# First norm's gain and bias applied beside the third and seventh expert tile, and the experts' load order computed ahead of the gates

## The chip, the cores and the metric

The kernel runs on one core of a Trainium2 chip. The metric is the device time of one execution in microseconds (us), from the first to the last instruction and what little lies around them. Engines are named as in the profile: PE (TensorE, matrix products), DVE (VectorE), ACT (ScalarE), POOL (GpSimd), SP (SyncE, which issues the weight transfers). They run side by side and wait for each other only through semaphores.

## The reference

One layer of a decoder for 512 tokens of width 1024. Four mixing branches are gated and summed into `merged`, and then:

```python
        x = layer_norm(DEEPNORM_ALPHA * x + merged @ w_out[l], ln1_g[l], ln1_b[l])

        y = hierarchical_moe(x.reshape(b * T, D_MODEL), r_group[l], r_group_b[l], r_expert[l],
                             r_expert_b[l], e_gate[l], e_up[l], e_down[l])
        x = layer_norm(DEEPNORM_ALPHA * x + y.reshape(b, T, D_MODEL), ln2_g[l], ln2_b[l])
```

`layer_norm` subtracts the mean, divides by the root of the variance plus 1e-5, and applies a row of gains and a row of biases. `hierarchical_moe` picks one of 4 expert groups for each token and in it the best 2 of 8 experts; an expert computes `silu(x @ w_gate) * (x @ w_up) @ w_down` with matrices of 1024 x 512, 1024 x 512 and 512 x 1024 in float32, and a token's two results are added with gate weights. All 32 experts are read, 6 MB each.

## The kernel before

The first 720 us or so compute the input projection, the four branches, the output product and the first norm. `x1`, which later is called `acc`, is a 512 x 1024 tile in SBUF (four blocks of 128 tokens); `normed` leaves in it the normed rows without gain and bias, and `xh` and `xl` hold the same numbers transposed, rounded (`xh`) and the rest (`xl`).

Then comes the expert stage (`moe`). The experts are worked on in 13 tiles of 128 slots. Tiles 0 and 1 hold the fixed experts 0 to 3, 64 slots each; tiles 2 to 12 are filled by the table `TILES` (rank of an expert by its number of tokens, and its slots), so which expert stands where is known only once the tokens are counted. `router` works that out: it ranks the 28 other experts by their counts (`rkey`, `rsq`, `rrank`), finds each token's slot, and writes the list of experts in the order of the tiles, `R.order` (`rord`). SP reads this list into registers (`num`, line 1188) before it can issue a weight transfer for tile 2 or later.

Weights come in transfers of 1 MB, which I number through: an expert has 6 (two each of gate, up, down), so tile 0 has transfers 0 to 11, tile 1 has 12 to 23, tile 2, with four experts, 24 to 47. There are 16 buffers; transfer n goes into buffer n mod 16 and so waits until PE has read transfer n - 16. All are issued by SP in this order (line 1753), and SP also waits at line 1753 for landings of earlier ones.

A tile is one call of `expert_block`: gate products `pg`, up products `pu`, `hh` = silu(pg) * pu (ACT, then DVE), four transposes, down products `py` from `hT`; `yh` (ACT) and `yl` (DVE) are py scaled and split; `combine` spreads them to the token rows with a one-hot matrix and adds the result to `acc` (DVE, line 1148). A tile's two combines run inside the next tile (`mid` after the gate products, and `late` after hT). `early` and `late` are hooks ahead of and behind the transposes: in tile 0, `early` computes the gates (`gates`, `slot_gates`), then `affine`, and `late` runs `rest`, that is `router`. Every second tile gathers the token columns for the next two (`Gather`, lines 1058 and 1060, into `xe`) with one-hot matrices `D` from the slots.

`affine` turns `acc` into ALPHA * (gain * x + bias): four DVE instructions of 128 x 1024 (line 1873), one ACT instruction (1875), four POOL instructions of 128 x 1024 (1877). Its rows `g1` and `b1` are broadcast to 128 partitions by two transfers of 512 KB from POOL's queue. They stand at the end of `early` in tile 0, so on DVE ahead of tile 0's `hh`, and `router` stands behind it. Instructions are recorded and put in order per engine by a scheduler; `issue_after` holds a group back until an instruction named is issued.

Of the kernel before, what the change touches and what calls it, by code (L numbers as in the profile page):

```python
# [17 lines left out]
P = 128  # L18
# [691 lines left out]
def branch_a(K, st, q, k, v1, v2, v3, emit):  # L710
# [62 lines left out]
    for ct in range(2):  # L773
# [128 lines left out]
def gates(K, R):  # L902

    V, A = K.nc.vector, K.nc.scalar
    sb = K.rwk
    s4 = lambda n: sb.tile([P, 4], F32, name=n)
    bc = lambda t, n: t.unsqueeze(2).to_broadcast([P, 4, n])
    gl = R.lg[:, :, 0:4]
    gm, m1, m2 = (R.m[:, i] for i in range(3))
    ge = sb.tile([P, 4, 4], F32, name="rge")  # L910
    V.tensor_tensor(ge, gl, bc(gm, 4), op=OP.subtract)
    A.activation(ge, ge, AF.Exp)
    gs = s4("rgs")
    V.tensor_reduce(gs, ge, axis=AX.X, op=OP.add)
    e2 = s4("re2")
    V.tensor_tensor(e2, m2, m1, op=OP.subtract)
    A.activation(e2, e2, AF.Exp)
    den = s4("rden")
    V.scalar_tensor_tensor(den, e2, 1.0, gs, op0=OP.add, op1=OP.mult)
    R.g = [K.rsb.tile([P, 4], F32, name=f"rgt{j}") for j in range(2)]  # L920
    V.reciprocal(R.g[0], den)
    V.tensor_tensor(R.g[1], R.g[0], e2, op=OP.mult)


def router(K, R):

    nc = K.nc
# [10 lines left out]
    V.scalar_tensor_tensor(key, cnt[:, ds_], float(NE), K.iof[:, ds_], op0=OP.mult, op1=OP.subtract)  # L938
    sq = sb.tile([P, ND, ND], F32, name="rsq", tag="rsq", bufs=1)
    V.tensor_tensor(sq, key[:, None, :].to_broadcast([P, ND, ND]), key.unsqueeze(2).to_broadcast([P, ND, ND]),  # L940
                    op=OP.is_gt)
    rank = row("rrank", ND)
    V.tensor_reduce(rank, sq, axis=AX.X, op=OP.add)

    at = lambda: V.tensor_tensor(sq, rank[:, None, :].to_broadcast([P, ND, ND]),
                                 K.plan[:, 0].unsqueeze(2).to_broadcast([P, ND, ND]), op=OP.is_equal)
    at()
    V.tensor_tensor(sq, sq, K.plan[:, 1].unsqueeze(2).to_broadcast([P, ND, ND]), op=OP.mult)
    V.tensor_reduce(key, sq.rearrange("p q e -> p e q"), axis=AX.X, op=OP.add)

    base, cap = row("rbase"), row("rcap")
    V.tensor_scalar(base[:, 0:NS], K.iof[:, 0:NS], float(CAP), None, op0=OP.mult)
# [33 lines left out]
    V.tensor_tensor(o8, over.unsqueeze(2).to_broadcast([P, NE, 8]), K.thr[:, None, :].to_broadcast([P, NE, 8]),
                    op=OP.is_gt)
    V.tensor_reduce(nbk, o8, axis=AX.X, op=OP.add)
# [88 lines left out]
            self.evac(h, xe)  # L1077


def expert_block(K, xe, gts, w, ex, out_acc, parts=((0, T), (T, DM)), done=None, spare=None, mid={}, fill=()):  # L1080

# [55 lines left out]
    def combine(i, c0, c1, yh, yl):  # L1137
        for b in range(NB):
            ps = psm.tile([P, c1 - c0], F32, name="pm", padded_shape=[P, T])
            TE.matmul(ps, DT[:, b, :], yh, start=True, stop=False)  # L1140
            end = TE.matmul(ps, DT[:, b, :], yl, start=False, stop=True)  # L1141
            o = out_acc[:, b, c0:c1]
            if spare is not None and (b, i) in POOLED:
                s = spare[0][:, POOLED.index((b, i)) % 8, 0:c1 - c0]
                A.copy(s, ps)  # L1145
                G.tensor_tensor(o, o, s, op=OP.add)  # L1146
            else:
                V.tensor_tensor(o, o, ps, op=OP.add)  # L1148
# [29 lines left out]
    nc.vector.tensor_tensor(lo, src, hi.bitcast(F32), op=OP.subtract)  # L1178


def moe(K, xh, xl, out_acc, R, d0, affine, rest, load, load_rows, load_cols, small, last, ews):

# [76 lines left out]
    for pr, tl in enumerate(tiles):  # L1259
# [233 lines left out]
def layer_kernel(tc, a, out):  # L1493
# [12 lines left out]
    with top:  # L1506
# [362 lines left out]
        K.osb = K.rsb  # L1869

        def affine():
            for b in range(NB):
                V.scalar_tensor_tensor(acc[:, b, :], acc[:, b, :], ALPHA, g1, op0=OP.mult, op1=OP.mult)
            with tc.issue_after(K.xend):
                A.mul(b1, b1, ALPHA)
            for b in range(NB):
                G.tensor_tensor(acc[:, b, :], acc[:, b, :], b1, op=OP.add)
            rst.close()

        def rest():  # L1880
            with ExitStack() as st:
                K.rwk = pool(st, "rw2")
                router(K, R)
# [63 lines left out]
```

## Time and profile before

| | us |
|---|---|
| median of 3 runs | 1215.8 (1214.27 to 1218.3) |
| the profiled execution | 1214.3 |
| its span | 1212.5 |
| PE busy | 1133.9 (94%) |
| DVE busy | 644.4 (53%) |
| ACT busy | 350.3 (29%) |
| POOL busy | 140.2 (12%) |

The profile is of one execution. Times inside it count from the first instruction; the execution's own time is 1.8 us more than its span. In the page's 40 slices the DMA engines are busy in changing amounts up to about 740 us and full from about 760 to 1180 us, at 420 GB/s or so. PE is busy almost throughout, which for pipelined products does not mean that it sets the pace. Weight transfers are asynchronous: SP issues them in order, and a transfer that can't be issued yet holds back all those behind it.

### The profile page before, as it was taken

What the parts mean: (1) busy time and instruction counts of PE and PEld (TensorE: products, weight loads), DVE (VectorE), ACT (ScalarE), POOL (GpSimd) and SP (SyncE); (2) the same over time, 40 slices, a digit from 0 to 9 for tenths busy, and PEclk for the clock granted to TensorE, in tenths of its full rate; (3) what the DMA queues carried; (4) which work ended last, traced back from release to release, by engine and by line L of the source; (5) the groups of instructions that cost most, each with busy time, mean ns of one, the idle gap of its engine ahead of it and who ended that gap; (6) DMA issues with size and microseconds to landing.
All of it is one profiled execution on the core that took longest, in us unless ns stands there. A gap on an engine that the chain in (4) does not pass through costs nothing.

```text
span 1212.5 us, 19047 instructions
## 1 busy us (share of the span) xinstructions
PE 1133.9 (94%) x7039; PEld 761.9 (63%) x7039; DVE 644.4 (53%) x1785; ACT 350.3 (29%) x752; POOL 140.2 (12%) x194
## 2 busy tenths in 40 slices
PE   8999999999999999999999988999999998898882
PEld 6768778888876667888888973533444442442431
DVE  6489788622248884343435589732444442243237
ACT  5434444433343544232334450100111110110012
POOL 4022232000000001111121134000000000000003
PEclk9999999999999999999999998999999998999996
DMA  7320230566561024555554256999999999999992
GB/s 189 84 56 18 54 89 19 157 190 193 179 182 36 18 82 154 169 178 173 160 163 129 71 178 281 415 421 421 420 421 420 420 422 421 420 422 420 421 378 79
DMA packets 108699, 276.65 MB, mean 228 GB/s; under 512 B 19393, under 2 KB 74780, under 8 KB 86076
## 3 DMA queue, kind: packets, MB, share of 16 engines
q1 hardware_dynamic: 90604, 252.79, 56.3%
q10 hardware_dynamic: 16768, 19.82, 5.1%
q0 software_dynamic: 1232, 2.81, 0.7%
q8 instruction: 56, 0.92, 0.3%
q14 instruction: 39, 0.32, 0.1%
HBM read 263.71 MB, written 11.67 MB: 227 GB/s over the span
## 4 chain that ended last, share of the span: by engine, by line
PE 59%; DMA 28%; DVE 9%; issue 1%; ACT 1%; POOL 1%; SPq 0%; ACTq 0%; DVEq 0%; POOLq 0%
DMA w<-in_e_gate 10%; PE mm L1404 9%; PE mm L1406 9%; PE mm L1405 9%; DMA w<-in_e_down 9%; DMA w<-in_e_up 8%; PE pu L1095 2%; PE pg L1095 1%; PE py L1125 1%; PE mm L1424 1%; PE mm L1426 1%; PE mm L1425 1%; PE po L1730 1%; PE po L1728 1%; PE po L1729 1%
## 5 line engine op out<-in xcount | busy, mean ns | idle before, releaser
L1178 DVE TENSOR_TENSOR wlo<-wraw,whi 128x512 fp32r<-128x512 f32 (+2 forms) x180 | 122.3, 683 | 201.2 <-ACT whi L1175 200.5
L1404 PE MATMUL mm<-xh,whi 128*128 128x512 f32 x496 | 198.1, 400 | 1.0 <-ACT whi L1175 0.7
L1405 PE MATMUL mm<-xl,whi 128*128 128x512 f32 x496 | 198.8, 401 | 0.0
L1406 PE MATMUL mm<-xh,wlo 128*128 128x512 f32 x496 | 198.0, 400 | 0.0
L1175 ACT CAST whi<-wraw 128x512 fp32r<-128x512 f32 (+2 forms) x180 | 109.7, 612 | 204.9 <-PE mm L1405 133.3
L1148 DVE TENSOR_TENSOR acc<-acc,pm 128x512 f32<-128x512 f32 (+1 forms) x106 | 64.2, 655 | 116.3 <-PE pm L1141 116.3
L1095 PE MATMUL pu<-w,xe 128*32 128x512 f32 (+1 forms) x576 | 108.0, 632 | 10.9 <-DMA w<-in_e_up 10.9
L1095 PE MATMUL pg<-w,xe 128*32 128x512 f32 (+1 forms) x576 | 103.7, 609 | 11.1 <-DMA w<-in_e_gate 11.1
L1125 PE MATMUL py<-w,hT 128*32 128x512 f32 (+2 forms) x608 | 107.4, 577 | 3.8 <-DMA w<-in_e_down 3.5
L1404 PEld LDWEIGHTS mm<-xh,whi 128*128 128x128 f32 x496 | 93.3, 188 | 26.1 <-issue 3.0
L1406 PEld LDWEIGHTS mm<-xh,wlo 128*128 128x128 f32 x496 | 93.3, 188 | 24.3 <-issue 3.6
L1405 PEld LDWEIGHTS mm<-xl,whi 128*128 128x128 f32 x496 | 93.3, 188 | 22.6 <-issue 2.7
L1095 PEld LDWEIGHTS pg<-w,xe 128*32 128x32 f32 (+1 forms) x576 | 30.7, 124 | 80.1 <-issue 57.4
L1095 PEld LDWEIGHTS pu<-w,xe 128*32 128x32 f32 (+1 forms) x576 | 29.8, 127 | 81.4 <-issue 60.6
L1125 PEld LDWEIGHTS py<-w,hT 128*32 128x32 f32 (+1 forms) x608 | 34.4, 123 | 67.9 <-issue 53.5
L1058 PE MATMUL pm<-D,xh 128*128 128x256 f32 (+1 forms) x224 | 53.9, 283 | 1.1 <-DVE D L1019 1.1
L1146 POOL TENSOR_TENSOR acc<-acc,yo 128x256 f32<-128x256 f32 x6 | 4.3, 732 | 434.0 <-ACT yo L1145 434.0
L1060 PE MATMUL pm<-D,xl 128*128 128x256 f32 (+1 forms) x224 | 53.8, 283 | 0.0
L1102 DVE TENSOR_TENSOR hh<-hh,pu 128x512 f32<-128x512 f32 x13 | 8.9, 686 | 81.1 <-PE pu L1095 81.1
L1735 POOL TENSOR_TENSOR mT<-mT,th 128x512 f32<-128x512 f32 x24 | 35.6, 1485 | 140.9 <-DVE th L1734 139.9
L1133 ACT ACTIVATE yh<-py,dg 128x512 fp32r<-128x512 f32 x24 | 16.5, 686 | 105.7 <-PE py L1125 88.6
L1426 PE MATMUL mm<-whi,xl 128*128 128x256 f32 (+1 forms) x160 | 46.3, 289 | 0.0
(639 smaller groups left out, 2005.2 us busy)
## 6 DMA issues: line engine op xcount, KB each, us to landing
w<-in_e_gate SPq DMA_DIRECT2D x60, 1024.0 KB, 19.8
w<-in_e_down SPq DMA_DIRECT2D x58, 1024.0 KB, 19.8
w<-in_e_up SPq DMA_DIRECT2D x58, 1024.0 KB, 19.8
wraw<-in_w_in SPq DMA_DIRECT2D x128, 256.0 KB, 3.1
w<-in_e_up SPq DMA_DIRECT2D x12, 512.0 KB, 15.7
w<-in_e_down SPq DMA_DIRECT2D x12, 512.0 KB, 8.5
wraw<-in_w_branch SPq DMA_DIRECT2D x16, 256.0 KB, 2.6
w<-in_e_gate SPq DMA_DIRECT2D x8, 512.0 KB, 5.4
```

The costliest lines, as they stand in the source:

```text
L1058: TE.matmul(ps[:, i, :], self.xh[:, kt, b * P:b * P + P], D[:, b, :], start=i == 0 and b == 0, stop=False, skip_group_check=True)
L1060: TE.matmul(ps[:, i, :], self.xl[:, kt, b * P:b * P + P], D[:, b, :], start=False, stop=i == per - 1 and b == NB - 1, skip_group_check=True)
L1095: end = TE.matmul(ps[c, :], xe[:, kt, c], w(e, kind, kt, 0, T), start=kt == 0, stop=kt == 7, skip_group_check=True)
L1125: TE.matmul(at(c0, c1)[c, :], hT[:, f, c], w(e, 2, f, c0, c1), start=f == 0 and c0 % T == 0, stop=f == 3 and c1 % T == 0, skip_group_check ...
L1148: V.tensor_tensor(o, o, ps, op=OP.add)
L1175: nc.scalar.copy(hi, src)
L1178: nc.vector.tensor_tensor(lo, src, hi.bitcast(F32), op=OP.subtract)
L1404: TE.matmul(ps[i], hi[:, k, cs], self.xh[:, kk, :], start=kk == 0, stop=False)
L1405: TE.matmul(ps[i], hi[:, k, cs], self.xl[:, kk, :], start=False, stop=False)
L1406: end = TE.matmul(ps[i], lo[:, k, cs], self.xh[:, kk, :], start=False, stop=kk == 7)
L1426: TE.matmul(ps[:, :n], self.xl[:, kk, s], hi[:, k, :], start=False, stop=kk == 7)
L1735: G.tensor_tensor(mT[:, j, :], mT[:, j, :], th, op=OP.add)
```

## The change

`affine` goes. The load order becomes a function of its own, `load_order`, which runs on DVE right behind the first gather's evacuation (`xe`) and ahead of the gates; `router` keeps the rest, its passes over 28 x 28 cut into two halves of 14 x 28. The first tile's combine writes `acc` with ACT copies in place of DVE additions (`first`). The residual ALPHA * (gain * x + bias) is added in two halves of columns by `residual`, in the `late` hooks of tiles 2 and 6: PE spreads gain and bias to 128 partitions in PSUM, DVE rebuilds x from `xh` and `xl`. Gain and bias are read as a tile of 8 x 256 (`gb8`), by two transfers of 4 x 256 on POOL's queue in place of the two broadcasts. The pool of the router's small tiles opens once, for both functions.

```diff
+RESIDUAL = (2, 6)
+
...
+def at_place(K, R, sq, places=slice(0, ND)):
+
+    K.nc.vector.tensor_tensor(sq, R.rank[:, None, :].to_broadcast(sq.shape),
+                              K.plan[:, 0, places].unsqueeze(2).to_broadcast(sq.shape), op=OP.is_equal)
+
+
+def load_order(K, R):
+
+    V = K.nc.vector
+    sb, keep = K.rwk, K.rsb
+    ds_ = slice(NS, NE)
+    key = sb.tile([P, ND], F32, name="rkey")
+
+    V.scalar_tensor_tensor(key, R.pos[:, 4, ds_], float(NE), K.iof[:, ds_], op0=OP.mult, op1=OP.subtract)
+    nh = ND // 2
+    sq = sb.tile([P, nh, ND], F32, name="rsq", tag="rsq", bufs=1)
+    R.rank = keep.tile([P, ND], F32, name="rrank")
+    for h in (slice(0, nh), slice(nh, ND)):
+        V.tensor_tensor(sq, key[:, None, :].to_broadcast([P, nh, ND]), key[:, h].unsqueeze(2).to_broadcast([P, nh, ND]),
+                        op=OP.is_gt)
+        V.tensor_reduce(R.rank[:, h], sq, axis=AX.X, op=OP.add)
+    for h in (slice(0, nh), slice(nh, ND)):
+        at_place(K, R, sq, h)
+        V.tensor_tensor(sq, sq, K.iof[:, None, ds_].to_broadcast([P, nh, ND]), op=OP.mult)
+        V.tensor_reduce(key[:, h], sq, axis=AX.X, op=OP.add)
+    R.order = keep.tile([P, ND], I32, name="rord")
+    K.oend = V.tensor_copy(R.order, key).ins
...
-    at = lambda: V.tensor_tensor(sq, rank[:, None, :].to_broadcast([P, ND, ND]),
-                                 K.plan[:, 0].unsqueeze(2).to_broadcast([P, ND, ND]), op=OP.is_equal)
-    at()
-    V.tensor_tensor(sq, sq, K.plan[:, 1].unsqueeze(2).to_broadcast([P, ND, ND]), op=OP.mult)
-    V.tensor_reduce(key, sq.rearrange("p q e -> p e q"), axis=AX.X, op=OP.add)
+    nh = ND // 2
+    sq = sb.tile([P, nh, ND], F32, name="rsq", tag="rsq", bufs=1)
+    k2 = row("rkey2", ND)
+    for o, h in ((key, slice(0, nh)), (k2, slice(nh, ND))):
+        at_place(K, R, sq, h)
+        V.tensor_tensor(sq, sq, K.plan[:, 1, h].unsqueeze(2).to_broadcast([P, nh, ND]), op=OP.mult)
+        V.tensor_reduce(o, sq.rearrange("p q e -> p e q"), axis=AX.X, op=OP.add)
+    V.tensor_tensor(key, key, k2, op=OP.add)
...
-    at()
-    G.tensor_tensor(sq, sq, K.iof[:, None, ds_].to_broadcast([P, ND, ND]), op=OP.mult)
-    V.tensor_reduce(key, sq, axis=AX.X, op=OP.add)
-    R.order = keep.tile([P, ND], I32, name="rord")
-    V.tensor_copy(R.order, key)
-
...
-            if spare is not None and (b, i) in POOLED:
+            if first:
+                A.copy(o, ps)
+            elif spare is not None and (b, i) in POOLED:
...
                 with tc.issue_after(d0[1].end.ins):
+                    load_order(K, R)
+                with tc.issue_after(K.oend):
                     gates(K, R)
...
-            if pr == 0:
-                with tc.issue_after(K.gend):
-                    affine()
...
+            if pr in RESIDUAL:
+                with tc.issue_after(after):
+                    residual(RESIDUAL.index(pr))
...
-        K.rwk = pool(rst, "rw1")
-        g1 = K.rwk.tile([P, DM], F32, name="g1")
-        b1 = K.mwk.tile([P, DM], F32, name="b1", tag="D", bufs=1)
-        row_bcast(nc.gpsimd, g1, a["ln1_g"][0])
-        row_bcast(nc.gpsimd, b1, a["ln1_b"][0])
+        K.rwk = pool(rst, "rw2")
...
-        def affine():
+        def residual(i):
+
+            gb = [K.psm.tile([P, T], F32, name="pm") for _ in range(2)]
+            for j in range(2):
+                for q in range(2):
+                    r = 4 * j + 2 * i + q
+                    TE.matmul(gb[j][:, 256 * q:256 * q + 256], K.ident[0:8, r:r + 1].to_broadcast([8, P]), K.gb8,
+                              start=True, stop=True)
             for b in range(NB):
-                V.scalar_tensor_tensor(acc[:, b, :], acc[:, b, :], ALPHA, g1, op0=OP.mult, op1=OP.mult)
...
+                for q in range(2):
+                    cs = slice(i * T + q * 256, i * T + q * 256 + 256)
+                    g_, b_ = (t_[:, q * 256:q * 256 + 256] for t_ in gb)
+                    t = K.mwk2.tile([P, 256], F32, name="rt", bufs=1)
+                    js = slice(b * P + 64 * i + 32 * q, b * P + 64 * i + 32 * q + 32)
+                    part = lambda x: x[:, :, js].bitcast(F32).rearrange("p k j -> p j k")
+                    V.tensor_tensor(t.rearrange("p (j k) -> p j k", k=8), part(xh), part(xl), op=OP.add)
+                    V.scalar_tensor_tensor(t, t, ALPHA, g_, op0=OP.mult, op1=OP.mult)
+                    V.tensor_tensor(t, t, acc[:, b, cs], op=OP.add)
+                    V.scalar_tensor_tensor(acc[:, b, cs], b_, ALPHA, t, op0=OP.mult, op1=OP.add)
+
...
```

What the engines get is shown at three places. On DVE behind tile 0's first gather (`xe` is its evacuation, `rord` the list that SP reads, `rge` the first instruction of the gates), before:

```order
L1071 TENSOR_SCALAR xe<-pm,ln1c 128x256 x4
L911 TENSOR_TENSOR rge<-lg,rm_6983 128x16
L916 TENSOR_TENSOR re_7933<-rm_6983 128x4
L914 TENSOR_REDUCE rgs<-rge 128x4
L919 SCALAR_TENSOR_TENSOR rden<-re_7933,rgs 128x4
```

and now:

```order
L1091 TENSOR_SCALAR xe<-pm,ln1c 128x256 x4
L940 SCALAR_TENSOR_TENSOR rkey<-rpos,iof 128x28
L945 TENSOR_TENSOR rsq<-rkey 128x392
L947 TENSOR_REDUCE rrank<-rsq 128x14
...
L929 TENSOR_TENSOR rsq<-rrank,plan 128x392
L950 TENSOR_TENSOR rsq<-rsq,iof 128x392
L951 TENSOR_REDUCE rkey<-rsq 128x14
...
L953 CAST rord<-rkey 128x28
L913 TENSOR_TENSOR rge<-lg,rm_6986 128x16
```

Twelve instructions have come between the evacuation and the gates, and `rord` is among them; the groups of two and three rows stand twice each.

Also on DVE, around tile 0's `hh` (`g` and `G` are the gate columns), before:

```order
L1035 TENSOR_TENSOR G<-G,g_7957 128x128
L1873 SCALAR_TENSOR_TENSOR acc<-acc,g_7870 128x1024 x4
L1033 TENSOR_SCALAR g_8169<-iof,rsl_6982,rgt_7938 128x128
L1102 TENSOR_TENSOR hh<-hh,pu 128x512
L938 SCALAR_TENSOR_TENSOR rkey<-rpos,iof 128x28
L952 TENSOR_SCALAR rbase<-iof 128x4
L953 MEMSET rcap 128x4
L940 TENSOR_TENSOR rsq<-rkey 128x784
```

and now:

```order
L1055 TENSOR_TENSOR G<-G,g_7972 128x128
L1053 TENSOR_SCALAR g_8167<-iof,rsl_6985,rgt_7953 128x128
L1123 TENSOR_TENSOR hh<-hh,pu 128x512
L929 TENSOR_TENSOR rsq<-rrank,plan 128x392
L978 TENSOR_SCALAR rbase<-iof 128x4
L979 MEMSET rcap 128x4
L973 TENSOR_TENSOR rsq<-rsq,plan 128x392
```

The four long `acc` instructions ahead of `hh` are gone, and the router begins with its second half of work.

On PE, in tile 1, where its up products meet the first combine of tile 0 (a row of `pu` or `pg` stands for two matmul records of the profile), before:

```order
L1095 MATMUL pu<-w_8104,xe 64x512
L1140 MATMUL pm<-yh,DT 128x512
L1141 MATMUL pm<-yl,DT 128x512
```

and now:

```order
L1116 MATMUL pu<-w_8098,xe 64x512
L1161 MATMUL pm<-yh,DT 128x512 x4
L1116 MATMUL pu<-w_8100,xe 64x512
L1116 MATMUL pu<-w_8098,xe 64x512
L1162 MATMUL pm<-yl,DT 128x512 x4
L1116 MATMUL pu<-w_8100,xe 64x512
```

Before, 11 of the 16 rows of `pu` stood ahead of the combine; now one stands ahead of its `yh` products and three ahead of its `yl` products. SP's list of transfers is the same in both.

## Rows read from the trace of the kernel before

**Rows 1.** Stretches of the stage: PE, PEld, DVE, ACT, POOL busy, PE's granted clock, DMA share, GB/s.

```profile
718.00:720.00 2.00, 1.23 (x11) 1.02 (x9) 1.86 (x9) 0.00 (x0) 0.51 (x1) 1.00 0.08 33
...
741.00:747.00 6.00, 5.75 (x18) 2.82 (x20) 6.00 (x11) 0.58 (x1) 1.83 (x1) 0.50 1.01 416
747.00:748.00 1.00, 1.00 (x6) 0.28 (x4) 1.00 (x3) 0.00 (x0) 0.00 (x0) 0.98 0.62 254
748.00:756.00 8.00, 8.00 (x40) 2.67 (x38) 8.00 (x22) 0.00 (x0) 1.84 (x1) 1.00 0.00 2
756.00:758.00 2.00, 2.00 (x12) 0.56 (x8) 1.97 (x11) 0.00 (x0) 0.00 (x0) 1.00 0.64 139
758.00:764.00 6.00, 5.75 (x27) 1.73 (x23) 6.00 (x33) 1.18 (x2) 0.00 (x0) 1.00 0.96 382
764.00:790.00 26.00, 24.89 (x154) 15.15 (x158) 16.37 (x38) 4.21 (x7) 0.00 (x0) 1.00 1.01 424
790.00:1179.00 389.00, 354.25 (x2084) 156.36 (x2076) 142.48 (x321) 39.68 (x65) 0.00 (x0) 0.98 1.02 418
1179.00:1213.00 34.00, 11.50 (x82) 7.90 (x80) 23.39 (x50) 7.82 (x18) 10.13 (x10) 0.72 0.27 100
```

**Rows 2.** What SP's queue waited for, 700 to 800: us in total, times, longest.

```profile
SPq L1188 <- DVE rlf L969: 18.0, 1, 18.0
SPq L1753 <- PE py L1125: 14.8, 2, 12.5
```

**Rows 3.** SP in order of time (start, length, transfers merged), around transfers 22, 24, 36.

```profile
736.40 0.80 SPq L1753 DMA_DIRECT2D w<-in_e_down  x2
755.71 2.53 SPq L1753 DMA_DIRECT2D w<-in_e_gate  x3
...
784.06 0.91 SPq L1753 DMA_DIRECT2D w<-in_e_up  x2
```

**Rows 4.** The page's list of DMA issues: KB each, us from issue to landing.

```profile
w<-in_e_gate SPq DMA_DIRECT2D x60, 1024.0 KB, 19.8
```

**Rows 5.** DVE in order of time: start, length, line, tiles, idle before it in brackets.

```profile
721.11 1.97 DVE L1071 TENSOR_SCALAR xe<-pm,ln1c 128x256 f32<-128x256 f32 x4 [0.90 <-PE pm L1060]
...
725.24 0.17 DVE L914 TENSOR_REDUCE rgs<-rge 128x4 f32<-128x16 f32 x1 [2.01 <-ACT rge L912]
...
729.37 8.95 DVE L1873 SCALAR_TENSOR_TENSOR acc<-acc,g 128x1024 f32<-128x1024 f32 x4
738.24 2.36 DVE L1033 TENSOR_SCALAR g<-iof,rsl,rgt 128x128 f32<-128x128 f32 x1
740.52 0.67 DVE L1102 TENSOR_TENSOR hh<-hh,pu 128x512 f32<-128x512 f32 x1
741.12 1.76 DVE L938 SCALAR_TENSOR_TENSOR rkey<-rpos,iof 128x28 f32<-128x28 f32 x1
...
742.91 0.98 DVE L940 TENSOR_TENSOR rsq<-rkey 128x784 f32<-128x784 f32 x1
...
748.12 1.62 DVE L949 TENSOR_REDUCE rkey<-rsq 128x28 f32<-128x784 f32 x1
...
754.74 0.17 DVE L981 CAST rord<-rkey 128x28 int32<-128x28 f32 x1
...
763.53 0.73 DVE L1134 SCALAR_TENSOR_TENSOR yl<-py,dg,yh 128x512 fp32r<-128x512 f32 x1
```

**Rows 6.** PE in order of time, tiles 0 and 1.

```profile
729.34 7.04 PE L1095 MATMUL pu<-w,xe 128*64 128x512 f32 x32
...
741.25 1.13 PE L1107 MATMUL pm<-ident,hh 128*128 128x128 f32 x4 [4.02 <-DVE hh L1102]
...
744.92 8.09 PE L1125 MATMUL py<-w,hT 128*64 128x512 f32 x32
...
769.72 0.75 PE L1107 MATMUL pm<-ident,hh 128*128 128x128 f32 x4 [0.78 <-DVE hh L1102]
```

**Rows 7.** The chain that ended last, 778 to 830: start, length, what.

```profile
780.45 7.02 PE py L1125 x32
...
792.75 16.65 DMA w<-in_e_down
```

More of the change, by code (lines that the diff above doesn't have):

```diff
@@ L937, in router @@
     key = row("rkey", ND)
[L938 to L943, printed above, removed]
-    at = lambda: V.tensor_tensor(sq, rank[:, None, :].to_broadcast([P, ND, ND]),
-                                 K.plan[:, 0].unsqueeze(2).to_broadcast([P, ND, ND]), op=OP.is_equal)
-    at()
-    V.tensor_tensor(sq, sq, K.plan[:, 1].unsqueeze(2).to_broadcast([P, ND, ND]), op=OP.mult)
-    V.tensor_reduce(key, sq.rearrange("p q e -> p e q"), axis=AX.X, op=OP.add)
+    nh = ND // 2
[6 more added lines that the diff above has]
+    V.tensor_tensor(key, key, k2, op=OP.add)
     base, cap = row("rbase"), row("rcap")
@@ L975, in router @@
         lf.append((l_, ov))
-    at()
-    G.tensor_tensor(sq, sq, K.iof[:, None, ds_].to_broadcast([P, ND, ND]), op=OP.mult)
-    V.tensor_reduce(key, sq, axis=AX.X, op=OP.add)
-    R.order = keep.tile([P, ND], I32, name="rord")
-    V.tensor_copy(R.order, key)
     nbk, over = row("rnbk"), row("rover")
     V.tensor_tensor(over, cnt, cap, op=OP.subtract)
-    o8 = sb.tile([P, NE, 8], F32, name="ro8", tag="rsq", bufs=1, padded_shape=[P, ND * ND // 8, 8])
+    o8 = sb.tile([P, NE, 8], F32, name="ro8", tag="rsq", bufs=1, padded_shape=[P, ND * ND // 16, 8])
     V.tensor_tensor(o8, over.unsqueeze(2).to_broadcast([P, NE, 8]), K.thr[:, None, :].to_broadcast([P, NE, 8]),
@@ L1077, in all, with expert_block @@
             self.evac(h, xe)
-def expert_block(K, xe, gts, w, ex, out_acc, parts=((0, T), (T, DM)), done=None, spare=None, mid={}, fill=()):
+def expert_block(K, xe, gts, w, ex, out_acc, parts=((0, T), (T, DM)), done=None, spare=None, mid={}, fill=(),
+                 first=False):
     nc, tc = K.nc, K.tc
@@ L1178, in split, with moe @@
     nc.vector.tensor_tensor(lo, src, hi.bitcast(F32), op=OP.subtract)
-def moe(K, xh, xl, out_acc, R, d0, affine, rest, load, load_rows, load_cols, small, last, ews):
+def moe(K, xh, xl, out_acc, R, d0, residual, rest, load, load_rows, load_cols, small, last, ews):
     nc, tc = K.nc, K.tc
@@ L1319, in moe @@
         prev = expert_block(K, xe[:, :, cs], gts, w, strips(tl), out_acc,
-                            **(dict(parts=LAST, done=done, spare=spare) if end else {}), mid=mid, fill=(early, late))
+                            **(dict(parts=LAST, done=done, spare=spare) if end else {}), mid=mid, fill=(early, late), first=pr == 0)
     overflow()
@@ L1675, in layer_kernel @@
         K.ln1c = K.rsb.tile([P, 2, 8], F32, name="ln1c")
+        K.gb8 = K.rsb.tile([8, T // 2], F32, name="gb8")
         for i, n in enumerate(("ln1_g", "ln1_b")):
+            nc.gpsimd.dma_start(out=K.gb8[4 * i:4 * i + 4, :], in_=a[n][0].rearrange("(r c) -> r c", r=4))
             nc.gpsimd.dma_start(out=K.ln1c[:, i, :], in_=a[n][0].rearrange("(p k) -> p k", p=P))
@@ L1869, in layer_kernel, with rest @@
         K.osb = K.rsb
-        def affine():
-            for b in range(NB):
-                V.scalar_tensor_tensor(acc[:, b, :], acc[:, b, :], ALPHA, g1, op0=OP.mult, op1=OP.mult)
[L1874 to L1877, printed above, removed]
+        def residual(i):
[5 more added lines that the diff above has]
+                              start=True, stop=True)
+            for b in range(NB):
+                for q in range(2):
[8 more added lines that the diff above has]
+                    V.scalar_tensor_tensor(acc[:, b, cs], b_, ALPHA, t, op0=OP.mult, op1=OP.add)
+        def rest():
+            router(K, R)
             rst.close()
[L1880 to L1883, printed above, removed]
             K.mwk2 = pool(top, "mwk2")
@@ L1922, in last @@
             return done, lambda: A.activation(root, K.eps, AF.Sqrt), (spare, ews[j].tile([P, 2 * DM], F32R, name="ye", tag=f"w{j}"))
-        moe(K, xh, xl, acc, R, (sl0, ga), affine, rest, load, load_rows, load_cols, small, last, ews)
+        moe(K, xh, xl, acc, R, (sl0, ga), residual, rest, load, load_rows, load_cols, small, last, ews)
 _INS = ['x', 'w_in', 'c_mu', 'c_w0', 'c_w2', 'c_a0', 'c_a2', 'c_g2', 'c_kk', 'c_ka', 'c_rk', 'c_gn_w', 'c_gn_b',
```

## The prediction

> **What bounds the kernel now.** I read the page's slices first: DMA full from 760 to 1180. So I cut the expert stage into stretches [rows 1]. The reader sees four things there. From 790 to 1179 the DMA engines move 418 GB/s without a break; a 1 MB transfer takes 19.8 us from issue to landing [rows 4], which at 2.49 us each (1.049 MB at 421 GB/s, about the mean of the two long stretches) is 8 transfers under way at a time. This stretch is the weights of tiles 2 to 12, and nothing but fewer bytes shortens it; the chain of waits turns from PE to DMA steps at 792.75 [rows 7]. From 748 to 756 the DMA engines stand still. Around the hole they are only partly fed: 254 GB/s in 747 to 748, 139 in 756 to 758, 382 in 758 to 764. And the end, 1179 to 1213, hangs on the last landing, so it moves with the stream.
>
> The hole is therefore worth its own length. In full-rate time it is 1.00 - 254/421 = 0.40, plus 8.00 - 0.04, plus 2 x (1 - 139/421) = 1.34, plus 6 x (1 - 382/421) = 0.56: 10.3 us in all.
>
> What makes it? SP's waits: 18.0 us at line 1188, the read of the load order, released by the router on DVE [rows 2]. SP had issued transfer 23 by 737.2 and issues transfer 24 at 755.71 [rows 3], right behind `rord` at 754.74 to 754.91 [rows 5]. The other long wait is 12.5 us for tile 1's `py` [rows 2], up to 784.06, when transfer 36 goes out [rows 3]: its buffer holds tile 1's first down weights. That one costs nothing now, since the stream is full around it [rows 1].
>
> `rord` is late because DVE is: `hh` waits behind `affine` (8.95 us) and a stretched gate column, from 729.37 to 740.52, though `pu` ended at 736.38 [rows 5, 6]. PE stands still 4.02 us for it [rows 6], and its granted clock in 741 to 747 is 0.50, the 1.2 GHz level [rows 1], so `py` takes 8.09 us where tile 1's takes 7.02 [rows 6, 7].
>
> **The change part by part.**
>
> Load order ahead of the gates: two key and cast instructions of about 0.2 us and ten on 392 elements. A pass over 784 takes 0.98 [rows 5], so half of it lies between 0.49 and, with a fixed part kept whole, some 0.55: 5.3 to 5.9 us in all. From the end of `xe` at 723.1 [rows 5] that puts `rord` at 728.4 to 729.0, while SP is busy issuing up to 737.2. The wait at line 1188 is then nothing. Behind it the gates move by the same 5.5 us, less what falls away of their 2.01 us wait for ACT [rows 5], which would now have its work ready. The gate columns, over by 729.4 before (the start of `acc`), end between 733 and 735. They stand ahead of `hh` on DVE, which can run at 736.4: 1.4 us or more to spare.
>
> `affine` gone: `hh` starts at once behind `pu`. As in tile 1, PE's transposes follow 0.78 us later [rows 6]: 737.2. From there to `py` it took 3.67 us at the lower clock (741.25 to 744.92); at full clock about 2.1. `py` runs 739.3 to 746.3. The first half frees the buffers of transfers 24 and 25 at 742.8, before the stream runs dry at 747 + 254/421 = 747.6. Transfers 24 to 35 then follow without a hole, if each buffer is free in time. They occupy 12 x 2.49 us, to 777.5.
>
> What is late next: transfer 36, which needs half of tile 1's `py`. From the end of tile 0's `py` (753.0) to the end of tile 1's `pu` (769.72 - 0.78 = 768.94) it is 15.9 us of PE at full clock [rows 6], and from there to the release at 784.06 another 15.1 [rows 3]. 746.3 + 15.9 + 15.1 = 777.3. So SP can issue it at 777.3, and the bytes come later: behind the issue at 755.71 the stretch from 756 to 758 moved what 0.66 us at full rate would (2 x 139/421), as if the stream had started at 757.34, 1.6 us behind the issue [rows 1, 3]. The stream would pause from 777.5 to 778.9, 1.4 us. The buffers behind it come free in the same order as before and as far apart.
>
> For that, `yl` must not be late: PE's list now has the first combine's `yl` products behind 3 of 16 rows of `pu`. Before, 22.4 us passed between the end of `hh` (741.1) and the start of `yl` (763.53) [rows 5]. Out of these go four of the router's passes at about 0.9 (3.6), the key at 1.76, and between 0 and 1.6 for a second column stretched beside POOL, like the 2.36 us one: 5.4 to 7.0. In come 0.7 for the halves and the first residual instruction, which stands ahead of `yl`, and 0.9 for the reduction that must wait for the transposes. From 737.1 that starts `yl` at 754.1 to 755.7, and it ends 0.7 later. PE wants it at about 754.3 (746.3, 26 gate records and 6 of `pu` at 7.02/32 = 0.22, four `yh` products at some 0.24): a wait of 0.5 to 2 us. Part of it is in the 15.9 already, since PE waited there for `yl` too; I add 0.5 and make the pause 1.9.
>
> ACT copies for tile 0: eight of 128 x 512, by DVE's `hh` of this shape 0.67 us each, on an engine busy 5.5% of 790 to 1179 (39.68 of 389) and little more before [rows 1]. Nothing.
>
> `residual`, twice: 32 DVE instructions of 128 x 256. By `hh` at 0.67 for 512 columns one is 0.34; the first of each four reads `xh` and `xl` with a stride, and the reduce that reads so took 1.62 against 0.98 for plain passes of the same size [rows 5], hence 0.56. Together 8 x (0.56 + 3 x 0.34) = 12.6 us, at most 18 if all are strided. DVE is busy 142 of 389 us there [rows 1], and PE takes `yl` only behind the next tile's gate products, some 14 us on. Four more PE products per residual: 0.22 us as in `py`, or twice that. I take nothing: eight transfers under way are 19.8 us of slack [rows 4].
>
> Sum: 10.3 - 1.9 = 8.4 us. Against the profiled execution, 1214.3 - 8.4 = 1205.9. The median of the three runs is 1.5 above that execution; I give the median: **1207.4**.
>
> The broadcasts of `g1` and `b1` leave 1 MB less to move. The rows give that nothing: between 718 and 720 the engines run at 33 GB/s [rows 1], so what was queued before had drained. The Trainium skill, DMA: Bandwidth & Descriptors, section Issuing engines are not separate DMA queues, says that transfers from all engines' queues share the same 16 DMA engines and interleave; by that alone the weights would gain what the broadcasts took. That is a rival.
>
> **The rivals.**
>
> *The broadcasts' bytes count.* 1.05 MB at 421 GB/s is 2.5 us earlier for the whole stream: 1204.9. Against it: the 33 GB/s.
>
> *PE lags in tile 1.* The clock falls again, or `yl` comes 2 to 5 us later than worked out; each such us delays transfer 36 by one. Gain 4 to 7: 1208.8 to 1211.8. For it: DVE is full from 741 to 764 [rows 1].
>
> *Only the order is early.* If `hh` does not move (gates that end late), `py` stays at 744.92 to 753 and frees buffer 24's half at about 749; bytes at 750.6, a hole of 3.0 us, and transfer 36, still at 784.06, leaves another of 785.7 - 780.5 = 5.2. Gain 2.1: 1213.7. The change would then not do what it says.
>
> *PE blocked in `pu` (the other side).* `yl` is the place: 13 of 16 rows of `pu` now stand behind it, 26 records of 0.22 or 5.7 us. If `yl` ends only at 764.3 as before, `pu` ends at 764.3 + 0.9 + 5.7 = 770.9, 2 us later than now, transfer 36 goes out at 786.1, the pause is 787.7 - 777.5 = 10.2, and the gain is nil. From there each us costs one; DVE 4 us slower than before gives 1219.7. Against it: the work taken from DVE.
>
> *The residual is too slow.* Should a residual hold DVE over 14 + 19.8 = 34 us, the stream would stop for it. That is 2.7 times my estimate; both at 42 would cost 16 us, 1223. The Trainium skill, SBUF — State Buffer, section Door 1: The DMA port swizzle, says that an access which leaves a 16-byte line pays a penalty, and these reads leave it with every element; the 1.62 us row agrees, at 1.65 times and not at more.
>
> **How the numbers follow.** A change under 0.3%, 3.6 us, can't be told from none here. Forecast (gain 7 to 10.3) 0.64; bytes 0.06; PE lags 0.14; only the order 0.10; blocked 0.04; residual 0.02. Faster is the first three, 0.84; same 0.10; slower 0.06. The range from 1204.5, beyond the bytes' 1204.9, to 1211.5 holds the first two and most of the third, 0.8.
>
> **What would show it.** In the changed profile: SP's read of `rord` waits for nothing, `rord` stands near 728.7, no stretch under 400 GB/s lies between 728 and 777; `hh` at 736.4 and PE's clock at 1.00 through 736 to 750; a short dip near 778; the stream's end near 1170. Wrong would be a hole that stays at 748, `yl` later than 756 with PE idle in `pu`, or a dip behind tile 2 or 6 with SP waiting for PE there.

## The result and the profile after

The changed kernel takes 1207.96 us, median of four runs (1206.44 to 1209.14), against 1215.76 (1214.27 to 1218.3, four runs) before: the ratio on record is 0.9933, with a 95% interval of 0.9913 to 0.9953. The forecast was 1207.4.

The two profiled executions, 1214.3 before and 1209.14 after, differ by 5.1 us only. The reason lies ahead of the place where the change works: tile 0's first gate product starts at 722.42 in the one and at 726.00 in the other. From there to the end of the execution it is 491.9 us before and 483.1 after. I call this stretch the **stage**; it is where the change works, and in it the gain is 8.7 us. What the start does is taken up with the experiments.

The same stretches of the changed kernel's profile as in [rows 1] (busy time of PE, PEld, DVE, ACT, POOL, PE's granted clock, DMA share, GB/s):

```profile
741.00:747.00 6.00, 6.00 (x32) 2.57 (x34) 5.84 (x18) 0.59 (x1) 0.00 (x0) 1.00 1.02 412
747.00:748.00 1.00, 1.00 (x6) 0.29 (x4) 1.00 (x8) 0.00 (x0) 0.00 (x0) 1.00 1.04 434
748.00:756.00 8.00, 8.00 (x39) 2.60 (x36) 8.00 (x43) 0.69 (x1) 0.00 (x0) 1.00 1.01 420
756.00:758.00 2.00, 2.00 (x8) 0.71 (x8) 2.00 (x8) 0.60 (x1) 0.00 (x0) 1.00 1.01 418
758.00:764.00 6.00, 5.90 (x28) 2.31 (x28) 0.84 (x2) 2.63 (x5) 0.00 (x0) 1.00 1.02 422
...
790.00:1179.00 389.00, 352.88 (x2096) 158.40 (x2090) 172.73 (x392) 41.33 (x69) 1.42 (x2) 0.98 1.01 415
1179.00:1213.00 34.00, 7.54 (x51) 5.07 (x46) 20.61 (x43) 6.23 (x14) 8.71 (x8) 0.70 0.18 65
```

The hole is gone: the 8 us that moved 2 GB/s move 420. PE's clock in 741 to 747 is 1.00 where it was 0.50. The end runs dry sooner (65 GB/s in 1179 to 1213, before 100). What the hole was worth is read from 22.0 to 44.0 us behind each kernel's own first gate product, first before and then after:

```profile
744.42:766.42 22.00, 21.43 (x92) 7.39 (x90) 21.37 (x72) 1.57 (x3) 1.84 (x1) 0.94 0.58 225
748.00:770.00 22.00, 21.02 (x99) 9.20 (x96) 11.53 (x52) 6.46 (x12) 0.00 (x0) 1.00 1.01 420
```

That is 22 x (420 - 225)/421 = 10.2 us of transfers. What is left of a pause stands further on, around transfer 36:

```profile
778.00:780.00 2.00, 2.00 (x12) 0.63 (x10) 2.00 (x9) 0.00 (x0) 0.00 (x0) 1.00 1.02 422
780.00:782.00 2.00, 2.00 (x12) 0.71 (x10) 2.00 (x8) 0.00 (x0) 0.00 (x0) 1.00 0.94 315
782.00:784.00 2.00, 2.00 (x12) 0.44 (x12) 1.94 (x6) 0.69 (x1) 0.00 (x0) 1.00 0.96 377
```

At 421 GB/s that is 2 x (1 - 315/421) + 2 x (1 - 377/421) = 0.7 us.

SP's waits, 700 to 800 (us in total, times, longest), for [rows 2]:

```profile
SPq L1781 <- PE py L1146: 23.1, 4, 14.2
...
SPq L1212 <- DVE rsq L929: 0.5, 1, 0.5
```

and its issues of transfers 24 and 36, for [rows 3]:

```profile
746.50 1.29 SPq L1781 DMA_DIRECT2D w<-in_e_gate  x2
...
780.25 0.91 SPq L1781 DMA_DIRECT2D w<-in_e_up  x2
```

The read of the load order waits 0.5 us in place of 18.0 (the profile puts it down to a later pass of the router; the list itself stood at 732.95, and SP had issued transfer 23 only at 740.78), and SP now waits for PE: transfer 24 goes out 20.5 us behind the first gate product (before 33.3), as soon as `py` has read its buffer, and transfer 36 at 54.25 (before 61.64).

DVE in order of time, for [rows 5]; the third row is one of ten of its kind in `load_order`:

```profile
725.15 1.50 DVE L1091 TENSOR_SCALAR xe<-pm,ln1c 128x256 f32<-128x256 f32 x3 [0.30 <-PE pm L1080]
726.57 0.18 DVE L940 SCALAR_TENSOR_TENSOR rkey<-rpos,iof 128x28 f32<-128x28 f32 x1
726.78 0.57 DVE L945 TENSOR_TENSOR rsq<-rkey 128x392 f32<-128x392 f32 x1
727.38 0.56 DVE L947 TENSOR_REDUCE rrank<-rsq 128x14 f32<-128x392 f32 x1
...
732.77 0.18 DVE L953 CAST rord<-rkey 128x28 int32<-128x28 f32 x1
...
733.31 0.17 DVE L916 TENSOR_REDUCE rgs<-rge 128x4 f32<-128x16 f32 x1 [0.21 <-ACT rge L914]
...
740.10 0.69 DVE L1123 TENSOR_TENSOR hh<-hh,pu 128x512 f32<-128x512 f32 x1 [2.19 <-PE pu L1116]
740.70 0.56 DVE L929 TENSOR_TENSOR rsq<-rrank,plan 128x392 f32<-128x392 f32 x1
741.18 0.16 DVE L978 TENSOR_SCALAR rbase<-iof 128x4 f32<-128x4 f32 x1
...
757.36 0.74 DVE L1155 SCALAR_TENSOR_TENSOR yl<-py,dg,yh 128x512 fp32r<-128x512 f32 x1
```

and PE, for [rows 6]:

```profile
726.00 7.09 PE L1116 MATMUL pg<-w,xe 128*64 128x512 f32 x32
732.92 7.04 PE L1116 MATMUL pu<-w,xe 128*64 128x512 f32 x32
...
740.84 0.75 PE L1128 MATMUL pm<-ident,hh 128*128 128x128 f32 x4
...
742.87 7.04 PE L1146 MATMUL py<-w,hT 128*64 128x512 f32 x32
...
758.15 1.19 PE L1162 MATMUL pm<-yl,DT 128*128 128x512 f32 x4
```

DVE sits 2.19 us idle ahead of `hh`, which comes 0.14 us behind the end of `pu` (739.96); before, PE waited 4.02 us for it. The `yl` products come 0.10 us behind the products ahead of them (758.05).

### The profile page after: what moved, and what is told of

Its sections match the earlier page's. It is cut to its first block, busy times and chain, and to the rows that moved or that the text cites. A ratio compares the mean times of both kernels' runs of the same rounds, so it can differ in the third digit from the quotient of the medians.

```text
span 1207.4 us, 19153 instructions
## 1 busy us (share of the span) xinstructions
PE 1131.1 (94%) x7055; PEld 762.2 (63%) x7055; DVE 656.8 (54%) x1847; ACT 353.9 (29%) x759; POOL 126.1 (10%) x189
## 4 chain that ended last, share of the span: by engine, by line
PE 66%; DMA 21%; DVE 7%; issue 2%; POOL 1%; ACT 1%; SPq 0%; ACTq 0%; DVEq 0%; POOLq 0%
PE mm L1430 8%; PE mm L1432 8%; PE mm L1431 8%; DMA w<-in_e_gate 8%; DMA w<-in_e_down 5%; DMA w<-in_e_up 5%; PE pu L1116 5%; PE pg L1116 4%; PE py L1146 3%; PE pm L1080 2%; PE pm L1078 2%; PE pm L1161 1%; PE pm L1162 1%; PE mm L1452 1%; PE po L1758 1%
## 5 line engine op out<-in xcount | busy, mean ns | idle before, releaser
L1171 DVE TENSOR_TENSOR acc<-acc,pm 128x512 f32<-128x512 f32 (+1 forms) x98 | 59.2, 653 | 97.4 <-PE pm L1162 97.4
L1116 PE MATMUL pg<-w,xe 128*32 128x512 f32 (+1 forms) x576 | 100.0, 595 | 10.1 <-DMA w<-in_e_gate 10.1
L1146 PE MATMUL py<-w,hT 128*32 128x512 f32 (+2 forms) x608 | 104.6, 579 | 3.2 <-DMA w<-in_e_down 2.9
L1078 PE MATMUL pm<-D,xh 128*128 128x256 f32 (+1 forms) x224 | 54.9, 287 | 0.0
```

The source lines that it names most:

```text
L1078: TE.matmul(ps[:, i, :], self.xh[:, kt, b * P:b * P + P], D[:, b, :], start=i == 0 and b == 0, stop=False, skip_group_check=True)
L1116: end = TE.matmul(ps[c, :], xe[:, kt, c], w(e, kind, kt, 0, T), start=kt == 0, stop=kt == 7, skip_group_check=True)
L1146: TE.matmul(at(c0, c1)[c, :], hT[:, f, c], w(e, 2, f, c0, c1), start=f == 0 and c0 % T == 0, stop=f == 3 and c1 % T == 0, skip_group_check ...
```

## The experiments

The theory: the gain is the hole, and it needs both halves of the change, the order for SP at 24 and the early `hh` for PE, because transfer 36 waits for tile 1's `py`. Since the start of tile 0 differs from execution to execution, each profile is read from its own first gate product, which the second column gives. The last column is the ratio to before on the same chip, over all runs of the kernel.

| profile | first gate product | execution | stage | ratio |
|---|---|---|---|---|
| before | 722.42 | 1214.3 | 491.9 | |
| before_again | 723.67 | 1215.61 | 491.9 | |
| after | 726.00 | 1209.14 | 483.1 | 0.9933 [0.9913, 0.9953] |
| after_again | 725.51 | 1208.63 | 483.1 | 0.9928 [0.9915, 0.9941] |
| order_alone | 727.91 | 1220.40 | 492.5 | 1.0009 [0.9998, 1.0019] |
| order_late | 723.98 | 1212.93 | 489.0 | 0.9975 [0.9964, 0.9987] |
| broadcasts_back | 723.83 | 1207.15 | 483.3 | 0.9919 [0.9906, 0.9933] |
| no_residual | 726.06 | 1209.76 | 483.7 | 0.9941 [0.9922, 0.9961] |
| rests_dve | 728.20 | 1211.55 | 483.4 | 0.9938 [0.9917, 0.9959] |
| order_behind_gates | 724.96 | 1208.24 | 483.3 | 0.9925 [0.9906, 0.9943] |
| yl_late | 724.20 | 1209.31 | 485.1 | 0.9944 [0.9926, 0.9963] |
| first_dve | 726.39 | 1210.03 | 483.6 | 0.9936 [0.9917, 0.9954] |

Where in the stream a gain arises and where it goes back is read from the landings of five transfers, counted from the first gate product: how much earlier than in the first profile of before, and at the end, the stage.

| landing of transfer | 26 | 35 | 36 | 44 | last of all | end |
|---|---|---|---|---|---|---|
| before, us behind the first gate product | 44.14 | 66.97 | 69.46 | 89.46 | 459.63 | 491.88 |
| earlier: after | 9.5 | 9.6 | 9.6 | 8.9 | 7.4 | 8.7 |
| earlier: after_again | 9.6 | 9.7 | 9.1 | 8.7 | 7.2 | 8.8 |
| earlier: order_late | 4.8 | 3.9 | 3.9 | 3.9 | 2.4 | 2.9 |
| earlier: order_alone | 4.0 | 3.9 | 1.1 | -0.2 | -1.9 | -0.6 |
| earlier: yl_late | 9.3 | 9.6 | 8.1 | 7.6 | 6.1 | 6.8 |

Single landings scatter: in before_again the 44th comes 1.0 us and the last 0.9 us later than in before. Between transfer 44 and the last one each of these five loses another 1.5 to 1.6 us. The long stretch shows it, first before and then after, 800 to 1100:

```profile
DMA packets 17321, 126.26 MB, mean 421 GB/s; under 512 B 1922, under 2 KB 1922, under 8 KB 1922
DMA packets 17250, 125.76 MB, mean 419 GB/s; under 512 B 1912, under 2 KB 1912, under 8 KB 1912
```

Both profiles of before move 421 GB/s there and all ten others 419, 0.5 to 0.6 MB or 1.2 to 1.3 us less. order_alone and no_residual are among the ten, so it is neither the residual nor the missing `affine`; the cause is open. What comes behind the last landing has become shorter by 0.5 to 1.4 us, which is open too.

**The order alone** (`order_alone`): the broadcasts and `affine` are back, `residual` and `first` are off.

```diff
-RESIDUAL = (2, 6)
+RESIDUAL = ()
...
+            if pr == 0:
+                with tc.issue_after(K.gend):
+                    K.affine()
```

> The load order ahead of the gates, but affine kept at its old place, no residual. Theory (both halves are needed): the order's 6.4 us push the gates, affine and hh on DVE; less the 2 us wait for ACT that they swallow, hh comes 4.4 us later than before, near 745. Tile 0's py then frees transfer 24's buffer near 753.4, so the hole shrinks only from 10 to some 7 to 8 us, and tile 1's py and transfer 36 come 4 us later: 1216 to 1220, no gain or a loss of up to 4 us. SP's wait for the order is gone, its wait for py in its place. Rival (the order alone does it, the rest is ornament): the hole goes, 1208 to 1209. The prediction's arithmetic for this case, with an hh that does not move: 1213.7.

Measured: 1218.43, ratio 1.0009, no gain. DVE and PE around `hh`:

```profile
739.36 8.93 DVE L1902 SCALAR_TENSOR_TENSOR acc<-acc,g 128x1024 f32<-128x1024 f32 x4
748.20 0.67 DVE L1123 TENSOR_TENSOR hh<-hh,pu 128x512 f32<-128x512 f32 x1
```

```profile
748.93 1.13 PE L1128 MATMUL pm<-ident,hh 128*128 128x128 f32 x4 [4.50 <-DVE hh L1123]
```

`hh` moves: it stands 20.3 us behind the first gate product, before 18.1 (740.52 - 722.42), half of the 4.4 us expected. PE waits 4.50 us for it and its clock falls again (0.61 in 748 to 756). Transfer 24 is 4.1 us earlier than before, but transfer 36 goes out at 791.31, 63.4 behind the start against 61.6, and what was won at 26 (4.0) is lost by 44 (-0.2). The theory's 1216 to 1220 holds.

**The order late** (`order_late`): the changed kernel, with the list computed in the router behind `hh`, by the same halves.

```diff
+    order_rows(K, R)
...
-                    load_order(K, R)
-                with tc.issue_after(K.oend):
                     gates(K, R)
...
+            load_order(K, R)
             router(K, R)
```

`order_rows`, called inside `router`, is the second half of the list's passes.

> The changed kernel with the load order computed inside the router again, behind hh (same halves of 392). Theory: hh is early (PE's clock stays 1.00), but rord comes some 14.5 us behind hh, so SP waits for it again (8 to 13 us) and the stream runs dry for 5 to 6 us: 1212 to 1214.5. Rival (taking affine off DVE is all that matters): within 1 us of the changed kernel, 1207.5 to 1209. Rival (the order is all that matters): no gain, 1215 to 1216.

Measured: 1214.74, ratio 0.9975, a gain of 3 us. `hh` and PE's clock are as in the changed kernel, but SP's waits (700 to 800) have this row again, and the engines starve:

```profile
SPq L1223 <- DVE g L1064: 13.8, 1, 13.8
```

```profile
748.00:756.00 8.00, 8.00 (x40) 2.72 (x38) 8.00 (x40) 1.17 (x2) 0.00 (x0) 1.00 0.36 121
```

That is 5.7 us at full rate (8 x (1 - 121/421)), the 5 to 6 expected; the time is 0.2 us above the range. By the stage, one half of the change alone brings nothing and the other 3 us; together they bring 8.7.

**The order behind the gates** (`order_behind_gates`): the call moves behind the gate columns.

```diff
-                    load_order(K, R)
-                with tc.issue_after(K.oend):
                     gates(K, R)
             gts.extend(slot_gates(K, sj, R.g, h * P))
+            if pr == 0:
+                with tc.issue_after(K.gend):
+                    load_order(K, R)
```

> The changed kernel with the load order behind the gates and their columns, directly ahead of tile 0's hh. Theory (what counts is that rord is there when SP has issued transfer 23, not its place ahead of the gates): the gates wait 2 us for ACT again, rord comes some 14 us behind the first gate product in place of 7, SP arrives at 14.8, hh moves by 0 to 1 us: a stage (first gate product to the end) of 483.1 to 484.3 us. Rival (it must stand ahead of the gates): hh 3 us late or more and a hole, 486 or more.

Measured: a stage of 483.3. `rord` stands at 738.27, 13.3 us behind the first gate product, and DVE still stands idle ahead of `hh` (0.61 us, waiting for `pu`). So the place ahead of the gates is not what counts; what counts is that the list is there when SP has issued transfer 23, and that nothing stands between `pu` and `hh`.

**The broadcasts back** (`broadcasts_back`), into tiles that nothing reads:

```diff
...
+        row_bcast(nc.gpsimd, g1, a["ln1_g"][0])
+        row_bcast(nc.gpsimd, b1, a["ln1_b"][0])
```

> The changed kernel with the two broadcasts of 512 KB put back on POOL's queue, into tiles that nothing reads. Theory: the engines have drained them before tile 0's weights are wanted, so nothing: within 0.6 us of the changed kernel. Rival (their bytes count): 2.5 us slower, near 1210.5. Rival (the broadcasts' place in POOL's queue sets when POOL meets DVE in the first norm): the first gate product moves from 726 back to 722.4 and the time falls by 3 us, near 1205.

Measured: a stage of 483.3 and nearly the same median, 1207.99. The first gate product stands at 723.83, between the 726 and the 722.4 of the second rival, and the time did not fall to its 1205; the start is taken up below. Their bytes show where there was room for them: from 714 to 726 this kernel moves 212 GB/s and the changed one 124, 12 us x 88 GB/s = 1.06 MB more. The Trainium skill (DMA: Bandwidth & Descriptors, Issuing engines are not separate DMA queues) says that transfers from every queue share the 16 DMA engines; the trace agrees, as POOL's queue moves 0.98 MB in this window beside the weights. But the engines then run dry (0 GB/s from about 718 to 721), so there the sharing costs the stage at most the 0.2 us between 483.3 and 483.1, and the 2.5 us of that rival are not there.

**No residual** (`no_residual`), **copies on DVE** (`first_dve`):

```diff
-            if pr in RESIDUAL:
-                with tc.issue_after(after):
-                    residual(RESIDUAL.index(pr))
```

```diff
             if first:
-                A.copy(o, ps)
+                V.tensor_copy(o, ps)
```

> The changed kernel with both residuals left out, so that gain, bias and the skip term of the first norm are missing from the result. Theory: DVE's 14 us for each lie beside a stream that has eight transfers under way, so the stage takes 483.1 us again, within 0.5. Rival (the residual holds PE or SP in tiles 2 and 6): 1 to 4 us faster.

> The changed kernel with tile 0's eight copies into acc on DVE in place of ACT. Theory: DVE has room around tile 1's hh, so nothing: a stage of 483.1 us within 0.5. Rival (the copies' place on ACT is a part of the gain): 484 to 486.

Measured: stages of 483.7 and 483.6, against 483.1. Both are 0.5 to 0.6 us longer, at the edge of the half microsecond that the expectations allowed. So the residual has no price that leaving it out would give back, and the copies' place on ACT is worth 0.5 us at most; where these 0.5 us come from isn't shown. In the changed kernel the residual takes this on DVE (instructions grouped, 790 to 1179: busy us, mean ns of one | idle ahead):

```profile
L1910 DVE TENSOR_TENSOR rt<-xh,xl 128x256 f32<-128x256 f32 x15 | 10.8, 720 | 0.2
L1912 DVE TENSOR_TENSOR rt<-rt,acc 128x256 f32<-128x256 f32 x16 | 6.7, 421 | 0.3
L1913 DVE SCALAR_TENSOR_TENSOR acc<-pm,rt 128x256 f32<-128x256 f32 x16 | 6.7, 420 | 0.3
L1911 DVE SCALAR_TENSOR_TENSOR rt<-rt,pm 128x256 f32<-128x256 f32 x16 | 6.7, 416 | 0.2
```

That is 8 x (0.72 + 3 x 0.42) = 15.8 us each, and it lies beside the stream.

**A late `yl`** (`yl_late`): tile 0's first `yl` is written ten times.

```diff
+        for _ in range(9 if first and c0 == 0 else 0):
+            V.scalar_tensor_tensor(yl, at(c0, c1), dg, yh.bitcast(F32), op0=OP.mult, op1=OP.subtract)
```

> The changed kernel with tile 0's first yl written ten times in place of once, so 6 to 7 us later; PE's yl products stand behind all of tile 1's up products in this program, hh ahead of the second half. Theory: PE wanted yl at the moment it came, so 6 us more would block PE if its list were the same; here the list gives way and only hh of tile 1, behind the extra writes on DVE, can come later: a stage of 483 to 484.5 us, transfer 36 at 54 to 55.5 us behind the first gate product. Rival (the prediction's: each us that yl is late delays transfer 36 by one): 489 us, transfer 36 at 60.

Measured: a stage of 485.1, 2.0 us more, between the two. With all of `pu` ahead of it, PE still waits:

```profile
763.90 1.20 PE L1164 MATMUL pm<-yl,DT 128*128 128x512 f32 x4 [1.65 <-DVE yl L1157]
```

and tile 1's `py` starts at 777.00, 52.8 us behind the first gate product (after: 776.58, 50.6). So PE is 2.2 us late, but transfer 36 goes out 1.4 us later (55.64 behind the start, after 54.25): in this program two of tile 1's down products stand ahead of the gather. The last weights land 1.2 us later than in the changed kernel, and the rest of the stage's 2.0 us arises behind them. That each us costs one, as the prediction had it for transfer 36, is therefore not shown. The order of sizes is what the theory had, a little outside its ranges, and far from the rival's 489 and 60. `yl` itself was 7.5 us late (38.9 us behind the start against 31.4), so the reordered list took up most of it. The prediction's slower rival counted on a list that stays as it is.

**Chance or change at the start** (`after_again`, `before_again`, both unchanged; `rests_dve`):

> The changed kernel unchanged, profiled once more. If the late start of tile 0 (first gate product at 726.0 where before had 722.4) is chance, a race of a tenth of a microsecond between POOL and DVE at 707, this profile has a good chance to show 722 to 723 with an execution near 1206; if it comes from the change, 726 stands again and the execution is near 1208 to 1209.

> The kernel before, profiled once more. Theory: the stage from tile 0's first gate product to the end took 491.9 us in the first profile of before (722.42 to 1214.27) and 483.1 to 483.3 in the three profiles with the whole change, and that is the change; where the first gate product stands is set further up, by whether DVE or POOL comes first near 707, and is chance. So the stage is 491.5 to 492.5 again, and the first gate product is likelier to stand at 724 to 727 than at 722.4, with an execution of 1216 to 1218. Rival (the change made the start later): 722.4 and 1214.3 again.

The stage repeats within 0.1 us in the two profiles of either kernel, so a median gives the usual start: before 1215.76 - 491.9 = 723.9 and, on the chip of after_again, 1217.74 - 491.9 = 725.8; after 1207.96 - 483.1 = 724.9 and 1208.68 - 483.1 = 725.6. The differences are 1.0 and -0.2. By its own expectation the one profile of after_again (725.51) spoke for the change, and before_again came out a little earlier than forecast; I follow the medians, which rest on more executions: the change doesn't make the start late by the 3.6 us of the first pair, in which 722.42 is the earliest of all twelve. A smaller delay they can't exclude.

One cause of the spread shows at the third block's norm. DVE and POOL, in before_again and then in after_again:

```profile
706.65 0.17 DVE L873 TENSOR_TENSOR rg<-rg,lg 128x8 f32<-128x8 f32 x1
706.85 1.50 DVE L876 SCALAR_TENSOR_TENSOR rel<-rg,lg 128x32 f32<-128x32 f32 x1
```

```profile
706.69 1.60 POOL L1825 TENSOR_TENSOR xl<-acc,xh 128x512 fp32r<-128x512 f32 x1 [5.91 <-DVE rg L870]
```

```profile
706.76 1.63 POOL L1853 TENSOR_TENSOR xl<-acc,xh 128x512 fp32r<-128x512 f32 x1 [5.86 <-DVE rg L872]
```

```profile
706.78 1.64 DVE L875 TENSOR_TENSOR rg<-rg,lg 128x8 f32<-128x8 f32 x1
708.45 1.46 DVE L878 SCALAR_TENSOR_TENSOR rel<-rg,lg 128x32 f32<-128x32 f32 x1
```

Where DVE comes first by 0.04 us its instruction takes 0.17; where POOL comes first by 0.02 it takes 1.64, POOL's own length. PE then waits 2.34 or 3.13 us for `rohs`. Who comes first goes with the kernel more than by chance: DVE does in both profiles of before and in yl_late, POOL in the eight other profiles in which POOL does this work (broadcasts_back among them, so the broadcasts don't decide it). From POOL's subtraction to the first gate product it is 15.4 to 17.0 us in those three and 17.1 to 18.8 in the eight. The next run takes POOL out:

```diff
-                G.tensor_tensor(xl[:, :, js], xb, xh[:, :, js].bitcast(F32), op=OP.subtract)
+                if b < 2:
+                    G.tensor_tensor(xl[:, :, js], xb, xh[:, :, js].bitcast(F32), op=OP.subtract)
...
+            if b > 1:
+                rests(b)
```

> The changed kernel with the last two blocks' xl subtraction on DVE in place of POOL. Theory (DVE waits 2.7 to 3.1 us behind each pair of POOL's subtractions, and PE's wait for rohs behind it takes its clock down): two DVE subtractions cost 1.4 to 2.8 us in place of that wait; the first gate product moves from 725.5 to between 722 and 724.5, the stage stays at 483.1 us: 1205 to 1207.5. Rival (the late start has another cause, or the strided subtraction is as slow on DVE): 725 to 726, 1208 to 1209.

Measured: 1209.11, ratio 0.9938: no gain. The place was missed: 728.20, since the work ahead already ran 4.5 us later (POOL's last subtraction of the second block at 703.83, in after_again at 699.33). On DVE one subtraction takes 1.09 to 1.19 us in place of the wait. So the collision is shown as a mechanism, and the lost race goes along with a start that is some 2 us later (by the means, 16.2 and 18.2); that it is the cause, what in the change tips the race, and what shifts the first 700 us by some us from one execution to the next stay open.

## Why the prediction was right

Times below count from the first gate product, the prediction's minus 722.42.

- **The hole, 10.3 us.** It went, and its size was right: 10.2 us by the bytes of 22.0 to 44.0. By landings it is less, 9.5 us at transfer 26 and 9.6 at transfer 35; what makes the difference between the two measures isn't shown.
- **The pause at transfer 36, 1.9 us.** Measured 0.7, and the landings agree (9.6 falls to 8.9 by transfer 44). Transfer 36 was forecast at 54.9 and went out at 54.25, and the 0.5 us added for a late `yl` were not needed (PE waited 0.10); together that is 1.1 of the 1.2 us.
- **The long stretch and the end, taken as unchanged.** They were not: the stretch lost 1.2 to 1.3 us (421 GB/s to 419), the last weights landed only 7.4 us earlier (8.1 between the second profiles), and the end behind them gave 0.7 to 1.4 us back. That 8.4 was forecast and 8.7 measured in the stage is thus partly luck: a pause too large and two terms that the sum doesn't have, one against the other. The medians differ by 7.8, that is 8.7 less what the start moved.
- **The load order, 5.3 to 5.9 us.** It took 6.4 (726.57 to 732.95). One pass is 0.56 to 0.57 where the sum had 0.49 to 0.55, and the ten start 0.60 apart, where each reads what the last one wrote or writes over what it read. Behind `hh` the same pass (740.70) is followed after 0.48 by an instruction that needs nothing of it. The sum had no term for that. It cost nothing: the gates' wait fell from 2.01 to 0.21, and DVE was idle ahead of `hh`.
- **`hh`, the transposes, `py`.** Forecast 14.0, 14.8 and 16.9 to 23.9; measured 14.1, 14.8 and 16.9 to 23.9, at clock 1.00.
- **`yl`.** Forecast 31.7 to 33.3, measured 31.4.
- **The residual, 12.6 us each and at most 18.** Measured 15.8, and the price nothing, as forecast. A plain instruction takes 0.42, more than half of `hh`'s 0.67 as the sum had it (0.34); the strided one takes 0.72 against its 0.56, 1.7 times the plain one. The page SBUF — State Buffer of the Trainium skill (Door 1: The DMA port swizzle) names the penalty, not its size; the trace agrees.
- **The copies on ACT and the broadcasts' bytes.** Nothing was forecast. The copies are worth 0.5 us at most, the bytes 0.2.
- **Only the order early, 1213.7.** The rival's condition, an `hh` that doesn't move, is not what the order alone does: 492.5 in place of a gain of 2.1. The prediction did not see that the order itself pushes `affine` and `hh`.
- **The start.** The prediction took it as given. The profile pair moved by 3.6 us there, the medians by 1.0 and -0.2, and the race at the third block's norm mostly falls against the changed kernel.

## What to carry to other kernels

A hole in a stream of transfers can have two causes in a row, here a list that came late and a buffer that was read late; taking away one shows little until the other goes too, so look for the next thing late before costing an edit. Compare two profiles from the point where the change begins to act: here that stretch repeats within 0.1 us, while the executions as a whole spread by 3 to 4 us. A chain of dependent instructions that is moved onto a path wants its start-to-start distance (0.60), not its duration (0.57). And a sum that comes out right is checked term by term: here the stretch that the change doesn't touch had lost 1.2 to 1.3 us, and the end had won 0.7 to 1.4.

## What the runs showed of the hardware

A DVE instruction of 128 x 8 that takes 0.17 us took 1.64 when it met a subtraction of POOL's that had started 0.02 us earlier, and the next, 128 x 32, took 1.46 beside the second one; both have two operands in SBUF. The Trainium skill (SBUF — State Buffer, SBUF: two separate sides) calls the port pair that the two engines share an exclusive lock, held for the whole instruction; the trace agrees, since the wait ends with POOL's instruction each time. This wait lies inside the instruction's own time and not ahead of it, so these two engines do not wait for each other through semaphores only, as the section on the chip has it. The granted clock behind it is not settled: after PE waits of 2.34 us it stayed at 1.00 in 711 to 714 in the first profile of before and was 0.50 in before_again.
